# Steps around the output projection of a hybrid attention layer placed anew, and its block sums moved from VectorE to GpSimd

## The chip, the core and the metric

The kernel runs on one core of a Trainium2 chip. The metric is the device time of one execution in microseconds (us). The core has five engines that run their own instruction queues beside one another and wait for each other by semaphores: TensorE (PE, matmuls and transposes; PEld is its weight load), VectorE (DVE), ScalarE (ACT), GpSimd (POOL) and SyncE (SP), which here does nothing but issue DMAs. POOL and ACT issue some DMAs too.

## The reference, cut to what matters

One decoder layer on 2048 tokens of width 1024, all float32. Two kinds of heads share one input projection: gated linear attention (GLA) and dilated sliding-window attention with three branches (window, dilation). Their outputs, side by side, go through the output projection `w_out`, which is where most of the change stands; a normalized MLP of width 4096 follows.

```python
def rmsnorm(x, g):
    return x * rsqrt(mean(x * x, -1) + EPS) * g

nx = rmsnorm(h, attn_norm_g)
gq, gk, gv, gr, glow, dq, dk_, dv_ = split(nx @ w_in)
glog = log_sigmoid(glow @ gla_gate_w2 + gla_gate_b) / 16
o_a = gla_mixer(gq, gk, gv, glog)                  # 4 heads, chunks of 64 tokens
o_a = rmsnorm(o_a, gla_norm_g) * silu(gr)
o_b = dilated_mixer(dq, dk_, dv_, rel_bias)        # 8 heads, (128,1) (512,4) (2048,16)
h = h + concat(o_a, o_b) @ w_out
nm = rmsnorm(h, mlp_norm_g)
h = h + square(relu(nm @ w_ff1)) @ w_ff2
return rmsnorm(h, final_norm_g)
```

## The kernel before, in words

**Arithmetic.** Each float32 operand of a large matmul is split into a high and a low part: ACT rounds the high part (L543), DVE subtracts it to get the low part (L544), and PE runs three matmuls (L140 to L142). A "split" below is this pair of instructions; PE cannot start on an operand before both have run. Many matrix products are done with Strassen-like products of quarter blocks, which need sums of blocks of the operands.

**Stages.** The input projection runs to about 503 us; then attention and GLA, interleaved, to about 849 us; then the output projection to about 1035 us, the first MLP product to about 1645 us and the second to the end.

**Attention and GLA.** The attention is cut into `units`; in each turn of the loop one unit computes scores (L982), DVE adds the bias and takes the row minimum (L992), ACT takes the exponential (L993), PE transposes (L1002), ACT copies (L1009), and PE multiplies with `v` (L1021). The queries of a head and branch are packed by POOL (`pack_q`, L935). `gla_steps` puts a GLA step between units: loads L1148 to L1150, matmuls L1175 and L1199, copies L1201 and L1212 on ACT, transposes L1211. Everything else that shall run meanwhile is listed with `at_unit(n, f, ...)`, which calls `f` at unit `n`.

**Preparation of the output weights.** `sum_wo(c)`, a generator, is called every second unit from unit 8 on, six times for each of four `c`: it loads two rows of blocks of `w_out` into a slot `wtsum` (L1275), has ACT scale one half by `gn`, the GLA norm's weights (L1277), then has POOL make four differences (L1281), and stores them to `wtD`. `mix_wo(c)` loads them again as `wtraw` (L1291) and splits them into four operands `wb`. `load_wo` loads other blocks as they are (`woraw`, L1265) and splits them.

**The output projection.** `mixD` in DRAM holds the attention outputs; `load_mix(p)` brings those of two blocks of 128 rows into `mx` (four DMAs, L1494), written by the last stores of combined attention (`cmb`, L1098 and L1110) and GLA. The first four blocks of 128 rows (`at` = 0 to 3, in the prediction block 0 to block 3, or the first to the fourth plain block) are computed without Strassen products: `plain_rows` splits their part of `mx` into `mT`, PE multiplies, DVE adds the residual `xh` (L1728). From `g` = 14 on, `product0(g)` runs seven products for each pair of blocks, with operands `mcomb` that `prep0` makes three products ahead (sums L1656 and its neighbours on DVE, then a split). `row_done` stores the new rows (L1664) and puts two kinds of entries on a list, `norms`; `next_norm` takes one entry at a time:

- `norm_row`: square-sum of the row by ACT (L1433, which writes its squares into `scr`, half of the one slot `gs`), the root (L174, L175), the scaled row by DVE into `scr` (L1435), eight transposes by PE (L1440), copies by ACT (L1441) into the slot `bb`, and stores to `hTD` (L1428). `scr` is one buffer: the next row's square-sum cannot start before this row's transposes have read it.
- `norm_sums`, after every second row: four differences of the 128x512 pieces in `bb` on DVE (L1448 to L1451), and four stores.

**What sets the order.** The program is traced in the order in which the code is written, and a list scheduler with a timeline of its own then orders each engine's queue; the code pins only a few instructions (`keep_in_program_order`). Buffers come from a pool of 25 rotating slots, so an allocation in another place can move other waits too. An engine runs its queue strictly in order: an instruction that waits holds all that stand behind it, and a DMA that waits on SP's queue holds the DMAs behind it.

## Time and profile before

| | before |
|---|---|
| median of 3 runs | 2224.94 us (2224.32 to 2226.07) |
| the profiled execution | 2224.69 us |
| its span, first to last instruction | 2222.9 us |
| mean granted TensorE clock | 0.994 |
| instructions in the span | 34722 |
| DMA traffic | 499.88 MB, 225 GB/s over the span |

The profile comes from one execution. In its rows, L12 is line 12 of the kernel; `out<-in` names the buffers that an instruction writes and reads; the bracket behind a row of the timeline gives the engine's idle time before it and what ended that. PE, DVE, ACT and POOL are busy time, which leaves out the issuing of DMAs. A granted clock of 1.00 is full speed of TensorE; at 0.50 the same matmul takes twice as long. Small gaps of a busy engine are found in the list of waits and in the windows, not in the shares of busy time: the whole span is 2222.9 us and the waits in question are of 1 to 4 us.

### The profile page before, as it was taken

How to read it: one execution, taken by the hardware profiler on the slowest of the kernel's cores; microseconds unless marked ns; L12 is line 12 of the kernel's file. 1: busy time of each engine (PE TensorE's matmuls, PEld its weight loads, DVE VectorE, ACT ScalarE, POOL GpSimd, SP SyncE). 2: the span in 40 equal slices, each digit the busy share in tenths (PEclk: the TensorE clock that was granted, in tenths of full speed). 3: DMA queues.
4: the chain of work that ended last, by engine and by line, in shares of the span. 5: the costliest groups of instructions: out<-in, count | busy, mean ns of one | idle time of the engine just before them, and what ended most of it. 6: DMA issues, size and time to landing. Idle time of an engine off the chain costs nothing.

```text
span 2222.9 us, 34722 instructions
## 1 busy us (share of the span) xinstructions
PE 2194.7 (99%) x12236; PEld 1905.9 (86%) x12236; DVE 1686.6 (76%) x3134; ACT 1227.1 (55%) x2388; POOL 609.5 (27%) x667
## 2 busy tenths in 40 slices
PE   9999999999999999999999999999999999999998
PEld 8988998899999997788788888888888888888886
DVE  8678766756787888779776778767787697576788
ACT  7365425537888884446555566555555433333446
POOL 1000300125577683000000000000008443042662
PEclk9999999999999999999999999999999999999999
DMA  6676966777967978978654456454489998687775
GB/s 211 178 219 208 249 202 187 250 232 265 305 221 218 282 241 234 281 246 268 192 159 140 146 172 195 151 180 154 134 294 279 306 295 268 217 267 236 268 262 183
DMA packets 341075, 499.88 MB, mean 225 GB/s; under 512 B 37703, under 2 KB 245210, under 8 KB 329636
## 3 DMA queue, kind: packets, MB, share of 16 engines
q1 hardware_dynamic: 300402, 332.88, 47.3%
q0 software_dynamic: 33152, 112.08, 17.9%
q10 hardware_dynamic: 7346, 52.70, 6.3%
q8 instruction: 96, 1.57, 0.3%
q14 instruction: 79, 0.65, 0.1%
HBM read 339.45 MB, written 162.85 MB: 226 GB/s over the span
## 4 chain that ended last, share of the span: by engine, by line
PE 74%; issue 15%; DMA 4%; DVE 4%; ACT 1%; POOL 1%; SPq 1%; POOLq 0%; DVEq 0%; ACTq 0%
PE ps_a L141 7%; PE ps_a L140 7%; PE ps_a L142 7%; PE ps_c L141 6%; PE ps_c L142 6%; PE ps_c L140 6%; PE ps_a L1021 4%; PE ps_d L141 4%; PE ps_d L140 4%; PE ps_d L142 4%; PE ps_o L140 3%; PE ps_o L141 3%; PE ps_o L142 3%; PE ps_d L1002 3%; PE ps_c L984 2%
## 5 line engine op out<-in xcount | busy, mean ns | idle before, releaser
L543 ACT ACTIVATE cb<-bs 128x1024 fp32r<-128x1024 f32 x104 | 110.2, 1060 | 284.5 <-PE ps_o L141 108.7
L544 DVE TENSOR_TENSOR cb<-bs,cb 128x1024 fp32r<-128x1024 f32 x104 | 158.4, 1524 | 123.3 <-ACT cb L543 122.8
L544 DVE TENSOR_TENSOR mcomb<-w1raw,mcomb 128x512 fp32r<-128x512 f32 x224 | 153.6, 686 | 98.4 <-ACT mcomb L543 98.4
L1819 POOL TENSOR_TENSOR bs<-bs,rb 128x1024 f32<-128x1024 f32 x60 | 165.7, 2763 | 200.2 <-DMA bs<-w_ff 195.2
L1535 POOL DMA_DIRECT2D w1raw<-w_ff x64 | 48.1, 752 | 592.5 <-DVE mcomb L544 565.7
L543 ACT ACTIVATE mcomb<-w1raw 128x512 fp32r<-128x512 f32 x224 | 140.2, 627 | 89.0 <-PE ps_c L142 26.5
L1021 PE MATMUL ps_a<-v,pt 128*128 128x65 f32 x1200 | 178.6, 256 | 4.4 <-ACT pt L1009 3.3
L1021 PEld LDWEIGHTS ps_a<-v,pt 128*128 128x128 f32 x1200 | 173.8, 196 | 6.7 <-ACT pt L1009 3.9
L993 ACT ACTIVATE pe<-pe,O 128x256 f32<-128x256 f32 (+1 forms) x384 | 155.4, 454 | 22.4 <-DVE O L992 20.9
L992 DVE CUSTOM_DVE_ANT_0 pe<-ps_c,nb 128x256 f32<-128x256 f32 (+1 forms) x384 | 125.6, 359 | 40.1 <-PE ps_d L1002 18.5
L1002 PE MATMUL ps_d<-ident,pe 128*128 128x128 f32 x600 | 154.9, 280 | 0.2 <-ACT pe L993 0.2
L304 ACT ACTIVATE wcomb<-wraw 128x512 fp32r<-128x512 f32 (+2 forms) x119 | 90.5, 761 | 114.4 <-PE ps_a L141 45.3
L544 DVE TENSOR_TENSOR ca<-ra,ca 128x1024 fp32r<-128x1024 f32 x84 | 134.2, 1598 | 0.1
L140 PE MATMUL ps_c<-hb,mcomb 128*128 128x512 f32 x320 | 124.5, 390 | 1.2 <-DVE acc L1621 1.2
L141 PE MATMUL ps_c<-hb,mcomb 128*128 128x512 f32 x320 | 124.5, 389 | 0.0
L142 PE MATMUL ps_c<-hb,mcomb 128*128 128x512 f32 x320 | 124.2, 389 | 0.0
L140 PE MATMUL ps_c<-cb,ca 128*128 128x512 f32 x312 | 121.4, 389 | 0.0
L141 PE MATMUL ps_c<-cb,ca 128*128 128x512 f32 x312 | 121.4, 389 | 0.0
L142 PE MATMUL ps_c<-cb,ca 128*128 128x512 f32 x312 | 121.4, 389 | 0.0
L306 DVE TENSOR_TENSOR wcomb<-wraw,wcomb 128x512 fp32r<-128x512 f32 (+2 forms) x77 | 72.8, 946 | 48.9 <-ACT wcomb L304 48.7
L1002 PEld LDWEIGHTS ps_d<-ident,pe 128*128 128x128 f32 x600 | 106.6, 184 | 0.7 <-ACT pe L993 0.3
L140 PE MATMUL ps_a<-wcomb,tb 128*128 128x256 f32 (+1 forms) x344 | 98.0, 285 | 0.0
(502 smaller groups left out, 7203.4 us busy)
## 6 DMA issues: line engine op xcount, KB each, us to landing
ra<-actD ACTq DMA_DIRECT2D x50, 1024.0 KB
actD<-ring SPq DMA_DIRECT2D x176, 256.0 KB
rb<-w_ff POOLq DMA_DIRECT2D x84, 512.0 KB, 6.4
bs<-w_ff SPq DMA_DIRECT2D x72, 512.0 KB
w1raw<-w_ff POOLq DMA_DIRECT2D x64, 512.0 KB, 5.1
k<-kD SPq DMA_DIRECT2D x16, 1024.0 KB
rb<-hTD SPq DMA_DIRECT2D x28, 512.0 KB
wraw<-w_in SPq DMA_DIRECT2D x48, 256.0 KB
```

What stands on the lines that cost most here:

```text
L140: T.matmul(out, sh, mh, start=first, stop=False, **kw)
L141: T.matmul(out, sl, mh, start=False, stop=False, **kw)
L142: T.matmul(out, sh, ml, start=False, stop=last, **kw)
L304: A.activation(hi, src, AF.Copy, scale=sc)
L306: V.tensor_tensor(lo, src, hi.bitcast(F32), op=OP.subtract)
L543: A.activation(hi, src, AF.Copy)
L544: V.tensor_tensor(lo, src, hi.bitcast(F32), op=OP.subtract)
L992: V.tensor_tensor_reduce(p, s, bias, scale=1.0, scalar=BIG, op0=OP.add, op1=OP.min, accum_out=nm)
L993: A.activation(p, p, AF.Exp, bias=nm, scale=-1.0)
L1002: T.transpose(pb[:, i * 128:i * 128 + 128], src, ident)
L1021: T.matmul(self.b.opsum[:, n % 4], self.pt[:, i * 128:i * 128 + 128], self.b.v[:, blk, cols], start=first, stop=last)
L1819: (engines or ((G,), (V, V))[len(sums) - 1])[e].tensor_tensor(v, v, r, op=OP.add if op == "+" else OP.subtract)
```

## The change

The numbers of instructions stay, apart from a few waits; 32 subtractions move from DVE to POOL. The parts are:

1. **Last output weights.** The raw blocks of `load_wo(6)` and `load_wo(7)` share one slot.
2. **`sum_wo`** has one more step between its loads and the scaling by ACT. At two units a step, the scaling now comes four units behind the loads instead of two, and the four generators together take 28 steps instead of 24.
3. **Queries.** Those of head 0, branch 1 are packed before the first unit, as those of branch 2 were.
4. **`load_mix(0)`** is called at unit `NU - 9` of the attention instead of behind all units; the functions that it needs are defined further up, unchanged.
5. **`turn_rows`.** The transposes, copies and stores of `norm_row` become a function of their own, called after the next product (or at the next `next_norm`, if that comes first).
6. **`norm_sums`** makes its four differences on POOL (`G`) instead of DVE (`V`).

The core of the diff:

```diff
--- before.py
+++ after.py
+    raws_wo = []
...
     def load_wo(c):
...
-            raw = slot("woraw")[:, :D]
+            if c < 7:
+                raws_wo[:] = [slot("woraw")]
+            raw = raws_wo[0][:, c // 7 * D:c // 7 * D + D]
             SP.dma_start(raw, wo[:, c])
...
     def sum_wo(c):
         raw = slot("wtsum")
         for k in range(2):
             SP.dma_start(raw[:, D * k:D * k + D], wo[:, c + 4 * k])
+        yield
         yield
         A.activation(raw[:, :D], raw[:, :D], AF.Copy, scale=gn[:, c:c + 1])
...
-    for part in range(4):
-        pack_q(0, 2, part)
+    for br in (2, 1):
+        for part in range(4):
+            pack_q(0, br, part)
...
-                for part in range(4) if first else ():
+                for part in range(4) if len(units) > 4 else ():
                     at_unit(first - 4 + part, pack_q, b.h, br, part)
...
     NU = len(units)
-    sums_wo = [x for c in range(4) for x in [sum_wo(c)] * 6]
+    sums_wo = [x for c in range(4) for x in [sum_wo(c)] * 7]
     for n, x in enumerate(sums_wo):
         at_unit(8 + AHEAD + 2 * n, next, x)
     for i in range(8):
         at_unit(NU - 28 + 3 * i + AHEAD, load_wo, (4, (1, 0), (12, 0), 5, (1, 1), (12, 1), 6, 7)[i])
+    at_unit(NU - 9 + AHEAD, load_mix, 0)
...
-    norms = []
+    norms, turning = [], []
...
     def norm_row(h, t):
...
         V.scalar_tensor_tensor(scr, h, r, gM, op0=OP.mult, op1=OP.mult)
-        k = t % HT // 4
-        for q in range(2):
-            pv = view(ps("c"), (4, 128))
-            for c in range(4):
-                T.transpose(pv[:, c], scr[:, (4 * q + c) * 128:(4 * q + c + 1) * 128], ident)
-            A.activation(hb4[2 * k + q], pv, AF.Copy)
-        store_T(t, *(((1, 0), (2, 1)) if k == 0 else ((3, 3),)))
+        turning.append(t)
+
+    def turn_rows():
+        while turning:
+            t = turning.pop(0)
+            k = t % HT // 4
+            for q in range(2):
+                pv = view(ps("c"), (4, 128))
+                for c in range(4):
+                    T.transpose(pv[:, c], scr[:, (4 * q + c) * 128:(4 * q + c + 1) * 128], ident)
+                A.activation(hb4[2 * k + q], pv, AF.Copy)
+            store_T(t, *(((1, 0), (2, 1)) if k == 0 else ((3, 3),)))
...
     def norm_sums(t, x):
         b11, b21, b12, b22 = hb4
         t2, t4, t3 = [view(v, (4, 128)) for v in (x[:, 0, :512], x[:, 0, 512:], x[:, 1, :512])]
-        V.tensor_tensor(b12, b12, b11, op=OP.subtract)
-        V.tensor_tensor(t2, b22, b12, op=OP.subtract)
-        V.tensor_tensor(t4, b21, t2, op=OP.subtract)
-        V.tensor_tensor(t3, t2, b11, op=OP.subtract)
+        G.tensor_tensor(b12, b12, b11, op=OP.subtract)
+        G.tensor_tensor(t2, b22, b12, op=OP.subtract)
+        G.tensor_tensor(t4, b21, t2, op=OP.subtract)
+        G.tensor_tensor(t3, t2, b11, op=OP.subtract)
...
     def next_norm():
+        turn_rows()
         if norms:
...
-    load_mix(0)
     nxt = plain_rows(0, 0)
     for at in range(4):
...
         next_norm()
+        turn_rows()
         row_done(p, e)
...
         product0(g)
+        turn_rows()
         if i in (0, 1, 5):
             next_norm()
...
         product1(at)
+        turn_rows()
         if at in (1, 2, 4):
             next_norm()
```

Three places show how the scheduler's order moves. In these rows the number is the line of the kernel, and xN counts equal rows.

SP's queue at the first loads of `sum_wo`, early in the attention (`nb` is a bias table of a branch, `qs`, `k` and `v` its operands); before:

```order
L913 DMA nb_4799<-rbD_110 128x256
L893 DMA v<-vD 128x16x128
L667 DMA qs<-qD_86 128x2048
L672 DMA k_5060<-kD_90 128x1x2048
L1275 DMA wtsum<-w_out 128x1024 x2
L672 DMA k_5130<-kD_90 128x1x2048
```

and now:

```order
L913 DMA nb_4804<-rbD_110 128x256
L893 DMA v<-vD 128x16x128
L1149 DMA gla<-gqD 128x2x128
L1150 DMA gla<-gkD 128x2x128
L667 DMA qs<-qD_86 128x2048
L913 DMA nb_4804<-rbD_110 128x256
L672 DMA k_5060<-kD_90 128x1x2048
L913 DMA nb_4804<-rbD_110 128x256
L1279 DMA wtsum<-w_out 128x1024
```

Two `gla` loads and two `nb` loads have moved ahead of the `wtsum` loads, which themselves are now parted by an `nb` load.

SP's queue from the last output weights to the second `mx`, at the border of attention and output projection; before:

```order
L1265 DMA woraw<-w_out 128x1024
L1110 DMA mixD_105<-gla 128x4x128
L1265 DMA woraw<-w_out 128x1024
L1494 DMA mx<-mixD_104 32x4x448 x4
L1517 DMA xh<-x 128x1024 x2
L1704 DMA gs<-mlp_norm_g 128x1024
L1494 DMA mx<-mixD_104 32x4x448 x2
L1517 DMA xh<-x 128x1024 x2
L1291 DMA wtraw<-wtD 128x1024 x2
L1110 DMA mixD_105<-gla 128x4x128
```

and now:

```order
L1269 DMA woraw<-w_out 128x1024 x2
L1110 DMA mixD_105<-cmb 2048x1x64
L1392 DMA mx<-mixD_104 32x4x448 x4
L1110 DMA mixD_105<-gla 128x4x128 x2
L1530 DMA xh<-x 128x1024 x2
L1717 DMA gs<-mlp_norm_g 128x1024
L1098 DMA mixD_105<-cmb 2048x1x32
L1392 DMA mx<-mixD_104 32x4x448 x2
L1530 DMA xh<-x 128x1024 x2
L1296 DMA wtraw<-wtD 128x1024 x2
```

The two `woraw` loads follow each other, the first four `mx` loads stand ahead of the GLA stores, and both GLA stores and a store of L1098 now stand ahead of the second `mx` and of the first `wtraw`.

ACT's queue at the third plain block (with buffer numbers: `xh_9778` before and `xh_9777` now hold the rows of the first two blocks, `mT_9869` and `mT_9868` are the third block's operand); before:

```order
L543 ACTIVATE wb5_9804<-wtraw_9801 128x512
L543 ACTIVATE wb6_9807<-wtraw_9801 128x512
L543 ACTIVATE wb4_9810<-wtraw_9801 128x512
L543 ACTIVATE wb7_9813<-wtraw_9801 128x512
L543 ACTIVATE mT_9869<-mx_9793 128x512
L543 ACTIVATE mT_9869<-mx_9793 128x384
L1433 ACTIVATE gs_9762,stats_80<-xh_9778 128x1024
```

and now:

```order
L1468 ACTIVATE gs_9766,stats_80<-xh_9777 128x1024
L174 ACTIVATE stats_80<-stats_80,pair_77 128x1
L175 ACTIVATE stats_80<-stats_80 128x1
L1468 ACTIVATE gs_9766,stats_80<-xh_9777 128x1024
L543 ACTIVATE wb5_9803<-wtraw_9800 128x512
L174 ACTIVATE stats_80<-stats_80,pair_77 128x1
L543 ACTIVATE wb6_9806<-wtraw_9800 128x512
L543 ACTIVATE wb4_9809<-wtraw_9800 128x512
L543 ACTIVATE wb7_9812<-wtraw_9800 128x512
L543 ACTIVATE mT_9868<-mx_9792 128x512
```

The square-sums of both rows of the first pair now stand ahead of the four `wb` splits and of the third block's `mT` split.

More of the change, by code (lines that the diff above doesn't have):

```diff
@@ L1375, in emit, with load_mix, mix_of, by_quarter @@
             was = b
+    tiles = [8 * half + i + 4 * k for half in range(2) for i in range(4) for k in range(2)]
+    mxs, xhs = {}, {}
+    def load_mix(p):
+        if p < 8:
+            u = mxs[p] = view(slot("mx"), (4, 512))
+            half, i = divmod(p, 4)
+            for g in range(4):
+                m = mixD[half][:, 4 * i + g]
+                n = 448 if half == 0 else 512
+                (SP, G)[g % 2 if p else 0].dma_start(u[32 * g:32 * g + 32, :, :n], bass.AP(
+                    tensor=m.tensor, offset=m.offset, ap=[[16 * 512, 32], [32 * 16 * 512, 4], [1, n]]))
+    def mix_of(p, e, q):
+        if q:
+            return mxs[p][:, :, 256:].rearrange("p g (c e t) -> p e c g t", e=2, t=32)[:, e]
+        return mxs[p][:, :, :256].rearrange("p g (e c t) -> p e c g t", e=2, t=32)[:, e]
+    def by_quarter(v):
+        return v.rearrange("p c (g t) -> p c g t", g=4)
+    def kept_on_chip(p):
+        if p < 4:
+            pv = ps("c")
+            for e in range(2):
+                T.transpose(pv[:, 128 * e:128 * e + 128], outs[3, 0][:, tiles[2 * p + e], 1:129], ident)
+            A.activation(mxs[p][:, :, 448:].rearrange("p g (e t) -> p e g t", e=2), view(pv, (2, 4, 32)), AF.Copy)
     NU = len(units)
-    sums_wo = [x for c in range(4) for x in [sum_wo(c)] * 6]
+    sums_wo = [x for c in range(4) for x in [sum_wo(c)] * 7]
     for n, x in enumerate(sums_wo):
@@ L1482, in token_pieces @@
         return step
-    tiles = [8 * half + i + 4 * k for half in range(2) for i in range(4) for k in range(2)]
-    mxs, xhs = {}, {}
-    def load_mix(p):
-        if p < 8:
-            u = mxs[p] = view(slot("mx"), (4, 512))
-            half, i = divmod(p, 4)
-            for g in range(4):
-                m = mixD[half][:, 4 * i + g]
-                n = 448 if half == 0 else 512
-                (SP, G)[g % 2 if p else 0].dma_start(u[32 * g:32 * g + 32, :, :n], bass.AP(
-                    tensor=m.tensor, offset=m.offset, ap=[[16 * 512, 32], [32 * 16 * 512, 4], [1, n]]))
-    def mix_of(p, e, q):
-        if q:
-            return mxs[p][:, :, 256:].rearrange("p g (c e t) -> p e c g t", e=2, t=32)[:, e]
-        return mxs[p][:, :, :256].rearrange("p g (e c t) -> p e c g t", e=2, t=32)[:, e]
-    def by_quarter(v):
-        return v.rearrange("p c (g t) -> p c g t", g=4)
-    def kept_on_chip(p):
-        if p < 4:
-            pv = ps("c")
-            for e in range(2):
-                T.transpose(pv[:, 128 * e:128 * e + 128], outs[3, 0][:, tiles[2 * p + e], 1:129], ident)
-            A.activation(mxs[p][:, :, 448:].rearrange("p g (e t) -> p e g t", e=2), view(pv, (2, 4, 32)), AF.Copy)
     def load_x(p, pin=False):
```

## The prediction

> **What bounds the kernel now.** The page comes first, then the list of what TensorE (PE) waited for, then windows round each of those waits.
>
> ```profile
> PE 2194.7 (99%) x12236; PEld 1905.9 (86%) x12236; DVE 1686.6 (76%) x3134; ACT 1227.1 (55%) x2388; POOL 609.5 (27%) x667
> ```
>
> PE is busy for 2194.7 of 2222.9 us. The change removes no matmul, so it can only win idle time of PE (28 us in all) and time at a lower clock. The wait list says where the idle time sits (total us, times, longest us):
>
> ```profile
> PE ps_a L1021 <- ACT pt L1009: 3.3, 3, 1.3
> PE ps_c L1440 <- DVE gs L1435: 3.2, 1, 3.2
> ...
> PE ps_o L1175 <- ACT gla L1212: 2.1, 1, 2.1
> PE ps_a L140 <- ACT mT L543: 1.6, 1, 1.6
> ...
> PE ps_c L982 <- POOL qp L935: 1.0, 1, 1.0
> PE ps_a L140 <- ACT mcomb L543: 0.7, 1, 0.7
> ```
>
> The windows (start:end, length, busy us of PE, PEld, DVE, ACT and POOL, granted clock, DMA share, GB/s) show what a wait costs beyond itself:
>
> ```profile
> 512.00:524.00 12.00, 12.00 (x114) 11.89 (x114) 9.80 (x42) 6.50 (x16) 4.82 (x8) 1.00 1.05 380
> 524.00:528.00 4.00, 2.72 (x27) 2.52 (x26) 1.63 (x7) 4.00 (x10) 2.86 (x3) 1.00 1.05 368
> 604.00:607.30 3.30, 1.18 (x7) 1.02 (x7) 1.04 (x5) 2.94 (x8) 1.72 (x2) 1.00 1.18 319
> 607.30:614.10 6.80, 6.80 (x32) 6.41 (x31) 3.48 (x10) 5.07 (x16) 5.96 (x9) 0.50 0.95 366
> 842.00:849.75 7.75, 4.03 (x33) 3.47 (x33) 5.12 (x9) 5.33 (x16) 2.43 (x6) 0.99 1.06 282
> 849.75:856.30 6.55, 6.52 (x19) 5.51 (x20) 5.95 (x18) 3.64 (x14) 4.70 (x10) 0.50 1.06 255
> 922.00:924.65 2.65, 0.44 (x2) 0.02 (x1) 2.65 (x5) 2.55 (x6) 0.00 (x0) 1.00 1.04 279
> 924.65:931.50 6.85, 5.86 (x18) 5.00 (x19) 4.71 (x7) 1.96 (x4) 0.00 (x0) 0.50 1.07 341
> ```
>
> After 2.1 us of idle (604), 3.7 us in pieces (842 to 849.75) and 3.2 us (922) the clock stands at 0.50 for some 6.8 us, which costs half of PE's busy time there: 3.4, 3.3 and 2.9 us. The 1.28 us of idle at 524 has no such stretch behind it. So the price of a wait is its length, and about 3.4 us more once it is long.
>
> By the Trainium skill ("TensorE: Matmul & The Clock Gate", Part 1: The HAM clock gate) the clock falls only after an idle window of about 3.4 us. The trace disagrees: 2.1 us was enough at 604. What this rule of the Trainium skill would give is part of the first rival.
>
> **The change part by part.** Times are those of the run before; signs are changes of the span.
>
> *Queries of head 0, branch 1, cast ahead.* At 509.7 PE waited 1.0 us (L982, above) for POOL's casts of these queries. They now run before the input projection ends, where POOL idles. **-1.0.**
>
> *The weight sums (`sum_wo`).* The extra step puts four instead of two units between a load and the ACT split that needs it. What stands behind a late split on ACT's queue is late with it. The first load, in the rows of SP, ACT and PE in the timeline:
>
> ```profile
> 514.04 1.25 SPq L1275 DMA_DIRECT2D wtsum<-w_out  x2
> 523.91 1.15 ACT L1277 ACTIVATE wtsum<-wtsum,stats 128x1024 f32<-128x1024 f32 x1 [3.74 <-DMA wtsum<-w_out]
> 524.97 1.19 ACT L993 ACTIVATE pe<-pe,O 128x256 f32<-128x256 f32 x3
> 526.68 0.44 PE L1021 MATMUL ps_a<-v,pt 128*128 128x65 f32 x2 [1.28 <-ACT pt L1009]
> ```
>
> The split still stands behind the 30th exponential, but two `gla` and two `nb` loads of 128 KB each (512 KB) have moved ahead of the load on SP. DMA is saturated here (380 GB/s, share 1.05, above), so it lands 1.4 us later, at 525.3. Behind the split now stand two exponentials and L1201, on which PE's L1211 waits: 1.06 for the split (524.97 - 523.91), 0.85 for the exponentials, 0.5 for L1201 and 0.1 for the hand-over put that at 527.8. PE reaches its wait at 526.68 - 1.28 = 525.4, less 1.0 for the casts, plus 0.4 (eight 128-column GLA matmuls more ahead of it, four score matmuls fewer): 524.8. Idle 3.0, and 0.4 more at the next L1021, against 1.28: +2.1; with the load no later than now +0.7. At 3 us I take the clock with it, as at 604: +3.4, or 0 if it holds. **+5.5** (0.7 to 5.5).
>
> The fourth load is the one behind the gap at 604 (first the chain of waits, then the timeline; the last two rows are the second load):
>
> ```profile
> 591.51 12.76 DMA wtsum<-w_out
> 604.36 1.15 ACT L1277 ACTIVATE wtsum<-wtsum,stats 128x1024 f32<-128x1024 f32 x1 [3.32 <-DMA wtsum<-w_out]
> 523.95 1.55 SPq L1275 DMA_DIRECT2D wtsum<-w_out  x2
> 531.24 1.15 ACT L1277 ACTIVATE wtsum<-wtsum,stats 128x1024 f32<-128x1024 f32 x1 [1.19 <-DMA wtsum<-w_out]
> ```
>
> It waited behind 2 MB of `qs` and `v` issued within the microsecond before. Now only `gla` loads stand right ahead of it; the `qs`, `v` and `k` are 9 us of matmuls earlier. The load at 523.95 took 7.3 us. ACT reaches the split 44 PE instructions (4.3 us) plus some 1.5 us after the queue moves on, 5.2 us after the issue; 3.4 us of matmuls less 1.6 us of ACT work cover 1.8 us more. So 7.0 us cost nothing and 7.3 cost 0.3 to 0.5. Both the 2.1 and the 3.4 go: **-5.0** (-5.5 to 0).
>
> *Shared slot of the last output weights and the early `load_mix(0)`.* The start of the output projection idles 3.7 us in pieces:
>
> ```profile
> 833.62 3.33 SPq L1265 DMA_DIRECT2D woraw<-w_out  x1
> ...
> 838.86 2.10 SPq L1494 DMA_DIRECT2D mx<-mixD  x4
> 841.16 1.06 ACT L543 ACTIVATE wo<-woraw 128x1024 fp32r<-128x1024 f32 x1 [2.19 <-DMA woraw<-w_out]
> ...
> 849.10 1.04 ACT L543 ACTIVATE mT<-mx 128x512 fp32r<-128x512 f32 x2 [1.29 <-DMA mx<-mixD]
> ```
>
> Before, the first `woraw` held SP for 3.3 us, then came a GLA store, the second `woraw` and `mx`. Now the second follows the first at once and the GLA store comes behind `mx`; I estimate that `mx` goes out 2.8 us earlier, near 836, held by the score matmul that frees its slot. The DMA share is 1.06, with the same bytes queued, so it lands 1.5 to 3 us earlier, at 846 to 847.6. The first `mT` matmul ran 0.7 us behind 849.1; without the 3.7 us of waits PE wants it at 846.0. GLA's L1199 stands behind both `mT` splits on ACT (0.9 us). I count 2.7 us left of 3.7, and the clock still falling: **-1.0** (-6.2 if `mx` lands by 845.5, so that 0.9 is left and the clock holds).
>
> What is late next is the third plain block. In program order on SP, `xh`, the second `mx` and `wtraw` now come behind the last GLA store and the L1098 store. On ACT, the square-sum of the second block (L1433, now L1468) has moved ahead of four `wb` splits and the `mT` split of the third block. It needs the last matmul of block 1 and the eight transposes after it, and PE's next matmul needs that `mT`. Prices:
>
> ```profile
> 869.10 1.06 ACT L1433 ACTIVATE gs<-xh 128x1024 f32<-128x1024 f32 x1 [3.63 <-DVE xh L1728]
> 870.06 0.19 ACT L1433 ACTIVATION_READ_ACCUMULATOR gs<-xh 128x1 f32 x1
> 871.60 1.15 ACT L543 ACTIVATE wb<-wtraw 128x512 fp32r<-128x512 f32 x2 [1.35 <-DMA wtraw<-wtD]
> 872.65 0.28 ACT L174 ACTIVATE stats<-stats,pair 128x1 f32<-128x1 f32 x1
> ```
>
> Start to start: 1.15 + four splits at 0.53 + 0.2 for L174 + 0.55 for `mT`, and 0.2 for two hand-overs: 4.3 us, then 0.1 for DVE's half. PE has nothing else: 4.4 us idle, longer than any gap now, so 3.4 us of clock: **+7.8** (4.4, if the clock holds, to 11, if `wtraw`, late in the same queue, lands 3 us after the square-sum).
>
> *`turn_rows` and the sums on POOL.* At 922 PE waited 3.2 us for the normalized row, since DVE had waited for `mx` and then ran sums and combines first:
>
> ```profile
> 920.02 0.69 DVE L1656 TENSOR_TENSOR mx<-mx 128x512 f32<-128x512 f32 x1 [2.73 <-DMA mx<-mixD]
> 525.14 1.27 POOL L1281 TENSOR_TENSOR wtsum<-wtsum 128x512 f32<-128x512 f32 x1 [8.17 <-ACT wtsum L1277]
> ```
>
> The transposes now stand a product (some 11 us of matmuls) later and 4 x 0.6 us of sums have left DVE: 3.2 + 2.9 go, **-6.1** (0 if another `mx` wait takes its place). The same sums take POOL 4 x 1.27 = 5.1 us a pair of blocks, in some 19 us in which it otherwise only issues DMAs. They have one cost: SP's seventh `wtraw` load now waits, in queue, behind a store of the third sum.
>
> ```profile
> 896.57 1.31 SPq L1291 DMA_DIRECT2D wtraw<-wtD  x2
> 902.55 1.15 ACT L543 ACTIVATE wb<-wtraw 128x512 fp32r<-128x512 f32 x2 [0.79 <-DMA wtraw<-wtD]
> ```
>
> From the end of block 2: transposes, copy and three sums 5.2, two stores 1.1, 5.9 in flight, two `wb` splits 1.1, `mcomb` 0.6: 13.9, and PE wants `mcomb` at 10.9 + 2.0 = 12.9. With DVE's half I take 1.5 us against today's 0.7 (L140 <- `mcomb`): **+0.8** (0 to 5 with the clock).
>
> **Sum:** -1.0 + 5.5 - 5.0 - 1.0 + 7.8 - 6.1 + 0.8 = +1.0. The profiled run took 2224.69 us (span 2222.9), 0.25 under the median of 2224.94; on the median's scale 2225.9. Gains of 13 and losses of 14 cancel: **no change that can be told**, and 0.2% (4.4 us) is about what a measurement of this kernel can tell from none.
>
> **The rivals.** *Faster: the clock holds and `mx` is in time.* The first load's gap stays without its 3.4 us, as the 1.28 at 524 did, and the start closes to 0.9: 2225.9 - 3.4 - 5.2 = 2217.3. For it: `mx` needs to gain only 3.6 us. Against it: 2.1 us was enough at 604. By that rule of the Trainium skill ("TensorE: Matmul & The Clock Gate", Part 1) both gaps, and the one at 604, would be too short; then only the third block (4.4 us) would lose it. Chance 0.30.
>
> *Slower: the fourth load is late again.* If it takes 9.1 us or more from issue to landing, as at 591 it took 12.8, PE idles 2.1 us behind the split and loses the clock as now: 5.0 comes back, 2230.9. It decides at 7.0 us and costs all of it from 9.1. For it: the first load took 9.9 us at 514. Against it: the `k` loads before it have 9 us to drain. Chance 0.23, a late `wtraw` at the third block (+3) included.
>
> *The change does not do what it says* for `load_mix(0)`: its slot is freed by a late score matmul, so it could go out no earlier than now. That is +1.0 on the forecast, 2226.9, and lies within it. Forecast: 0.47 in all.
>
> **How the numbers follow.** Within 0.2%: 0.47; faster: 0.30; slower: 0.23. The range reaches past the faster rival by 2 us and past the slower one by 3: 2215 to 2234. The forecast's own range is 2221.5 to 2229.
>
> **What would show it.** Right: a PE wait of 4 to 5 us on ACT's `mT` split some 22 us after the first `mT` matmul, with the clock at 0.50 behind it; 3 us behind the first `wtsum` split; none behind the fourth; no PE wait on the transposes; POOL near 650 us busy. Wrong: no such wait at the third block (then some 8 us faster), or a wait on the transposes still there.

## The result, and the profile after

The changed kernel took 2251.10 us (median of 6 runs, 2245.85 to 2256.43), the kernel before 2226.82 us (6 runs): ratio 1.011, 95% interval 1.0091 to 1.013. It is slower by some 24 us. The forecast was 2225.9 us, no change that can be told, with a range of 2215 to 2234.

The profiled execution took 2248.78 us, its span 2247.0 us against 2222.9. Its page gives the busy time of each engine:

```profile
PE 2199.3 (98%) x12236; PEld 1907.2 (85%) x12236; DVE 1681.3 (75%) x3102; ACT 1227.2 (55%) x2388; POOL 664.4 (30%) x699
```

PE has as many instructions as before, and 4.6 us more busy time; 2.8 us of that come from longer stretches at a lower clock. The rest of the 24.1 us is idle. PE's list of waits says where (total us, times, longest us):

```profile
PE ps_a L140 <- ACT mT L543: 6.4, 1, 6.4
PE ps_o L1175 <- POOL gla L1165: 5.6, 1, 5.6
PE ps_o L1211 <- ACT gla L1201: 3.9, 1, 3.9
PE ps_a L140 <- ACT mcomb L543: 3.6, 1, 3.6
PE ps_a L140 <- DVE O L1024: 3.3, 1, 3.3
PE ps_a L706 <- DMA acc<-attn_norm_g: 2.3, 1, 2.3
PE ps_c L1481 <- DVE gs L1470: 2.2, 2, 1.8
```

The first five lines were not there before, or not above 1.6 us. Windows round these five (start:end, length, busy us of PE, PEld, DVE, ACT, POOL, granted clock, DMA share, GB/s), the first two gaps, and what follows each of the five:

```profile
510.00:515.80 5.80, 0.17 (x3) 0.01 (x1) 1.11 (x5) 2.33 (x8) 2.77 (x6) 0.71 0.79 232
515.80:522.60 6.80, 6.80 (x45) 6.44 (x46) 3.13 (x12) 2.09 (x5) 2.17 (x4) 0.75 0.98 271
622.90:627.10 4.20, 0.30 (x4) 0.10 (x2) 0.87 (x6) 1.71 (x3) 3.02 (x6) 0.75 0.54 178
627.10:633.50 6.40, 6.40 (x37) 6.29 (x38) 3.20 (x11) 6.37 (x25) 4.89 (x6) 0.63 0.01 2
867.60:871.00 3.40, 3.37 (x8) 2.67 (x9) 3.40 (x8) 0.00 (x0) 0.00 (x0) 0.53 0.53 135
893.30:899.60 6.30, 6.29 (x18) 4.73 (x19) 4.89 (x9) 3.68 (x9) 0.00 (x0) 0.62 1.02 251
923.50:930.00 6.50, 6.50 (x18) 4.99 (x19) 6.34 (x12) 5.10 (x11) 1.09 (x2) 0.59 0.92 244
```

Behind each gap the clock is lower, but the loss there is 1.6 to 2.7 us (busy time times what is missing from 1), not 3.4: the clock already falls inside the longer gaps (0.71 at 510, 0.75 at 622.9), so part of the low stretch is spent idle, and behind the gap that ends at 867 the stretch is short. Narrower windows show a clock of 0.50 from 512.4 to 519.2, 625.0 to 631.9, 867.4 to 870.8, 891.3 to 898.1 and 922.0 to 928.8, and 1.00 on either side: 6.8 us each time and 3.4 once. In the four gaps of 3.6 to 6.4 us it began 1.9 to 4.4 us after PE went idle, so the loss does not follow the length of the gap.

The kernels can be laid beside one another by when PE reaches the same work. The table has, for the kernel before, the time in us at which PE starts the 101st and the 501st value matmul (L1021), the first matmul on `mT` and the first on `mcomb`, and the span; for the others the difference to it. "Border" is the loss between the last two matmuls. Up to 1.6 us of a column already stands at the first score matmul. e6 shows how far a column moves by itself: PE's order there is that of the kernel before, matmul for matmul, and its columns differ by up to 3.4 us.

| profiled execution | 101st value | 501st | first `mT` | first `mcomb` | span | border | ratio of times to before (95%) |
|---|---|---|---|---|---|---|---|
| before | 536.82 | 654.21 | 849.78 | 900.77 | 2222.9 | | |
| changed | +7.8 | +8.5 | +6.0 | +22.7 | +24.1 | +16.7 | 1.011 (1.0091 to 1.013) |
| e1 without early query casts | +1.3 | -2.4 | +9.6 | +18.1 | +20.8 | +8.5 | 1.0108 (1.0093 to 1.0123) |
| e2 without early `mx` | +9.7 | +14.9 | +11.7 | +15.5 | +21.0 | +3.8 | 1.0084 (1.0064 to 1.0103) |
| e3 without `turn_rows` | +8.1 | +8.9 | +5.9 | +22.1 | +24.3 | +16.2 | 1.0119 (1.0098 to 1.0139) |
| e4 sums on DVE | +8.1 | +9.4 | +6.1 | +17.3 | +18.8 | +11.2 | 1.0095 (1.0078 to 1.0112) |
| e5 early casts alone | +6.9 | +10.0 | +11.0 | +12.8 | +12.8 | +1.8 | 1.0091 (1.0068 to 1.0114) |
| e6 casts moved back | +2.5 | -2.2 | -2.6 | -3.4 | -2.7 | -0.8 | 1.0009 (0.9994 to 1.0024) |
| e7 early `mx` alone | +3.7 | +3.3 | +3.9 | +3.6 | +8.2 | -0.4 | 1.0012 (0.9999 to 1.0024) |
| e8 sums on POOL alone | +2.0 | -1.8 | -0.1 | -0.3 | +5.0 | -0.2 | 1.0033 (1.0021 to 1.0045) |
| e9 extra step alone | +1.1 | -2.0 | +7.0 | +5.9 | +9.8 | -1.2 | 1.005 (1.003 to 1.0069) |
| e10 `turn_rows` alone | +2.6 | -0.6 | -0.4 | -1.9 | -3.5 | -1.5 | 1.0007 (0.9995 to 1.0019) |
| e11 extra step, early `mx` | +3.6 | +3.4 | +15.9 | +28.9 | +36.6 | +12.9 | 1.0152 (1.013 to 1.0174) |
| e12 shared slot, early `mx` | 0.0 | -4.6 | -3.1 | -1.9 | +0.5 | +1.1 | 1.0005 (0.9991 to 1.002) |
| e13 changed, GLA stores by ACT | +8.4 | +7.1 | +4.8 | +7.0 | +12.8 | +2.2 | 1.0076 (1.0053 to 1.0099) |
| e14 changed, square-sums behind | +7.8 | +7.0 | +4.8 | +20.2 | +38.1 | +15.5 | 1.02 (1.0182 to 1.0218) |
| e15 without extra step | +9.4 | +17.7 | +20.1 | +27.7 | +33.6 | +7.7 | 1.0129 (1.0109 to 1.015) |
| e16 before, a spare slot | +2.3 | -1.0 | +6.1 | +5.8 | +7.1 | -0.3 | 1.0055 (1.0039 to 1.0072) |

The kernel before took 2220.5 to 2226.8 us in the different comparisons, so ratios are compared, and the columns are used for places, not for sums. Each row is one execution: those of e2, e7, e11 and e15 are the slowest of their runs (e7: 2232.88 us against a median of 2224.17), those of e14 and e16 the fastest. Against the changed kernel the intervals of e1 to e4, e13 and e15 overlap, so what a part costs there is read from its place in the trace, and the ratio is given beside it. The changed kernel has lost 7.8 us at the 101st value matmul (7.5 of them at the first), stays near that until the output projection, loses 16.7 us there before its first product, and little behind it.

### The profile page after: what moved, and what is told of

Same layout as the page of the kernel before. It is cut to its first block, busy times and chain, and to the rows that moved or that the text cites. A ratio compares the mean times of both kernels' runs of the same rounds, so it can differ in the third digit from the quotient of the medians.

```text
span 2247.0 us, 34732 instructions
## 1 busy us (share of the span) xinstructions
PE 2199.3 (98%) x12236; PEld 1907.2 (85%) x12236; DVE 1681.3 (75%) x3102; ACT 1227.2 (55%) x2388; POOL 664.4 (30%) x699
## 3 DMA queue, kind: packets, MB, share of 16 engines
q0 software_dynamic: 33152, 112.08, 17.7%
## 4 chain that ended last, share of the span: by engine, by line
PE 81%; DMA 7%; DVE 5%; ACT 2%; issue 2%; SPq 1%; POOL 1%; DVEq 0%; ACTq 0%; POOLq 0%
PE ps_a L140 8%; PE ps_a L141 8%; PE ps_a L142 8%; PE ps_c L141 7%; PE ps_c L140 7%; PE ps_c L142 7%; PE ps_d L141 4%; PE ps_d L142 4%; PE ps_d L140 4%; PE ps_o L140 4%; PE ps_o L141 4%; PE ps_o L142 4%; PE ps_a L1021 3%; PE ps_d L1002 2%; PE ps_c L984 1%
## 5 line engine op out<-in xcount | busy, mean ns | idle before, releaser
L544 DVE TENSOR_TENSOR mcomb<-w1raw,mcomb 128x512 fp32r<-128x512 f32 x224 | 158.1, 706 | 102.2 <-ACT mcomb L543 102.1
L1021 PE MATMUL ps_a<-v,pt 128*128 128x65 f32 x1200 | 178.2, 255 | 1.5 <-DVE pt L1011 0.9
L1021 PEld LDWEIGHTS ps_a<-v,pt 128*128 128x128 f32 x1200 | 172.8, 195 | 4.3 <-DVE pt L1011 2.6
L544 DVE TENSOR_TENSOR ca<-ra,ca 128x1024 fp32r<-128x1024 f32 x84 | 122.6, 1460 | 0.1
L1619 ACT ACTIVATE acc<-acc 128x512 f32<-128x512 f32 x96 | 60.6, 631 | 68.3 <-DVE acc L1638 27.6
```

Source lines behind the costliest of these rows:

```text
L544: V.tensor_tensor(lo, src, hi.bitcast(F32), op=OP.subtract)
L1021: T.matmul(self.b.opsum[:, n % 4], self.pt[:, i * 128:i * 128 + 128], self.b.v[:, blk, cols], start=first, stop=last)
```

## The experiments

**e1, the change without its third part.** Edit:

```diff
-    for br in (2, 1):
-        for part in range(4):
-            pack_q(0, br, part)
+    for part in range(4):
+        pack_q(0, 2, part)
...
-                for part in range(4) if len(units) > 4 else ():
+                for part in range(4) if first else ():
```

> The change without its third part: the queries of head 0, branch 1 are cast among the units again. Theory A (their early cast takes the slot in which the bias table nb stood, so that nb's first load waits for a matmul 47 instructions later, some 5.6 us, and every load behind it on SP is late): the wait of 5.6 us at 515.8 and its stretch at clock 0.50 go, the first load of nb goes out near 469.6 instead of 475.2; 8 us faster than the changed kernel, 2243. Theory B (the start is late because the extra step of sum_wo has moved GLA loads ahead of wtsum, as the prediction had it): a wait of 3 us behind the first wtsum split is there with or without the early casts; the time stays at 2251 or falls by 1 to 3 us.

In its place theory A held: the loss at the 101st value matmul is 1.3 us, not 7.8, and `nb` goes out at 470.5. But the time did not fall (1.0108): a new wait of 4.7 us stands at 782, where POOL's cast of a later head waits for its slot, which a store of `cmb` still reads. The timeline of POOL:

```profile
781.30 2.01 POOL L935 CAST qp<-qs 128x512 fp32r<-128x512 f32 x2 [6.05 <-DMA mixD<-cmb]
```

**e2, without its fourth part.** Edit: `load_mix(0)` behind the last unit again.

```diff
-    at_unit(NU - 9 + AHEAD, load_mix, 0)
...
+    load_mix(0)
     nxt = plain_rows(0, 0)
```

> The change without its fourth part: load_mix(0) stands behind the last unit again. Theory A (the early mx brings the first block's matmuls ahead of the attention's last GLA steps and combines, SP then holds xh, the second mx and wtraw behind a GLA store that leaves at 871, and PE waits at 867 for a bank of ps_a and at 893 for mT): both waits go (3.3 + 6.4, with 3.3 at a lower clock behind each) and some 3 to 6 us come back at the first mT matmul; 2251 - 16 + 5 = 2240. Theory B (the wait at 893 comes from turn_rows, whose transposes hold the second square-sum ahead of the mT split): the wait of 6 us on mT stays, only the 867 one goes; 2245 to 2248.

The border lost 3.8 us instead of 16.7, with no wait over 1.3 us on `mT`: theory A, in its place. The total fell by less than that (1.0084, an interval that overlaps the changed kernel's), since this kernel is 6 us later at the first `mT` matmul than the changed one; a wait of 5.3 us for L1201 stands in its attention.

**e3 and e4, without the fifth and without the sixth part.** Edits:

```diff
         turning.append(t)
+        turn_rows()
```

```diff
-        G.tensor_tensor(b12, b12, b11, op=OP.subtract)
+        V.tensor_tensor(b12, b12, b11, op=OP.subtract)
...
```

> The change without turn_rows: norm_row makes its transposes at once, as before the change. Theory A (turn_rows takes away the wait of the transposes for the normalized row, 3.2 us and 2.9 at a lower clock, and touches nothing else): that wait is back behind the first products; 2251 + 6 = 2257. Theory B (with the sums on POOL, DVE is early enough for the transposes, and turn_rows gains nothing): no wait on the transposes over 1 us; 2251.

> The change without its sixth part: the four differences of norm_sums on DVE again. Theory A (on POOL they cost 1.3 to 1.7 us each and their third store holds the seventh wtraw load on SP until 915.8, so PE waits 3.6 us for mcomb at 923 and loses 3 us of clock): that load goes out 2 to 3 us earlier, the wait falls to about 1 us or none, 2251 - 6 = 2245, if the transposes don't wait again. Theory B (beside the sums, DVE's own operations take twice as long, 1.36 against 0.68 us for a split, and PE pays for that all through the output projection): the time falls by 10 us or more, to 2241. Theory C (DVE is what the products wait for, and the sums on it bring the wait back): 2251 to 2256.

e3 came out as its theory B in time: `turn_rows` gains nothing here (1.0119 against 1.011); its waits on the transposes are 1.1 us at 946 and 1.8 at 1037, of which the changed kernel has the second too. e4 came out as A at its place: 5.4 us less at the first `mcomb` matmul, and the transposes did not wait again. But another `mcomb` wait of 2.9 us stands at 944, and the ratio of 1.0095 overlaps the changed kernel's.

**e5 and e6, the early casts alone.** Edits to the kernel before: the loop over `br` of the change, and, in e6, the same casts called behind the loop that loads `nb` and `v`.

> The kernel before with the third part of the change alone: the queries of head 0, branch 1 are cast ahead of the units, in the place where the change casts them. Theory A (their slot is the one in which nb stood, nb's first load waits 5.6 us longer): the first load of nb goes out 5 to 6 us later, PE waits some 5 us for L1175 behind POOL's copies of nb and loses 3 us of clock: 7 to 8 us slower than before (ratio 1.0035). Theory B (the start is late only together with the extra step of sum_wo): no such wait, 1 us faster or the same (ratio 0.9995 to 1.0).

> As e5, but the slot of these queries is asked for behind those of the three bias tables and the first v, so that nb keeps its slot; the casts still come ahead of the first unit. Theory A (slot order): nb's first load goes out as before the change, the wait at the start is gone, and so is the 1.0 us for the casts: ratio 0.999 to 1.0. Theory C (it is the eight casts in a row on POOL, 11 us, that delay the copies of nb behind them): the start is late as in e5, ratio 1.0035.

e5: theory A at the start (PE waits 4.7 us for L1175; SP's first `nb` load goes out at 475.2 instead of 469.2), and more than it: 1.0091, with waits of 1.7, 1.9 and 2.4 us later in the attention and 5.5 us for `mcomb`. One part alone makes most of the change's loss. e6 does not test its theories: its casts are late again, PE's order is that of the kernel before, and so is the time (2223.01 us, 1.0009, 0.9994 to 1.0024). It serves as a measure of how far the columns scatter.

**e7 and e8, the early `mx` alone and the sums on POOL alone.**

> The kernel before with the fourth part of the change alone: load_mix(0) at unit NU - 9. Theory A (the early load itself orders ACT and SP anew, so that block 2's mT split and its weights come late): a wait on mT of 4 us or more at the third plain block and 3 us of clock behind it, less the 3 to 6 us that the first mT matmul gains: 2 to 5 us slower than before (ratio 1.001 to 1.002). Theory B (it takes the later attention that the other parts cause to turn the early load into a loss, since there the first block's matmuls run ahead of the last GLA steps): here they don't, the start of the output projection gains 3 to 6 us and nothing is lost behind it: ratio 0.997 to 0.999.

> The kernel before with the sixth part alone: the four differences on POOL. Theory A (the store of the third one holds the seventh wtraw load on SP): PE waits 2.5 to 4 us for mcomb at the first product with the clock behind it, 5 to 7 us, and the transposes' wait of 3.2 us shrinks or stays: 0 to 6 us slower (ratio 1.0 to 1.003). Theory B (DVE beside POOL takes twice its time and PE pays all through the projection): 8 us slower or more (1.0035). Theory C (DVE is relieved of 2.4 us where the normalized row is late, and POOL has time): the transposes' wait goes with its clock, 4 to 6 us faster (0.9975).

e7 loses nothing at the border, but gains nothing either (1.0012, with an interval that includes 1): nearer to theory A's number, with B's picture. e8 is 1.0033: PE waits 2.0 us for `mcomb` instead of 0.7 and 1.6 us for the transposes instead of 3.2, as theory A has it; its span grows behind the first products, by 5 us, as theory B expected of it in kind; PE waits there 1.7 us for a normalized row at 1016, and 0.7 to 1.2 us for `mcomb` at 1044, 1062 and 1096.

**e9 and e10, the extra step alone and `turn_rows` alone.**

> The kernel before with the second part alone: the extra step of sum_wo. Theory A (as the prediction's two terms on sum_wo, with the sizes seen in e1: the fourth wtsum split comes in time and its 2.1 us with the clock go, while the first one costs PE no more than before): 3 to 6 us faster, ratio 0.997 to 0.999. Theory B (the extra step orders POOL's casts of a later head behind a store of cmb, as at 782 in e1, where PE waited 4.7 us and lost 3 us of clock): 8 us come on top: ratio 1.001 to 1.003.

> The kernel before with the fifth part alone: turn_rows. Theory A (the prediction's term: the transposes stand a product later and no longer wait for the normalized row at 922): 3.2 us and 2.9 us of clock go, ratio 0.9973. Theory B (the wait moves: the next square-sum, held by the transposes that now come later, makes the next row late, and a wait on the transposes or on mcomb takes its place): ratio 0.999 to 1.001.

e9: both theories in their places. The gap at 604 is gone (1.3 us late at the 251st value matmul, 1.4 early at the 451st, with a wait of 1.2 us for L1199 between them) and the first split costs 0.7 us instead of 1.3; but at 783 PE waits 5.7 us for a cast behind the store of `cmb`, and loses 9 us with the clock: 1.005. e10 has theory B's number, but not its mechanism: the wait of the transposes is not moved, it is still there. PE's and DVE's rows in e10:

```profile
918.67 0.69 DVE L1662 TENSOR_TENSOR mx<-mx 128x512 f32<-128x512 f32 x1 [2.71 <-DMA mx<-mixD]
924.29 1.03 PE L1474 MATMUL ps_c<-ident,gs 128*128 128x128 f32 x5 [3.38 <-DVE gs L1463]
```

The normalized row is late because DVE waits for `mx`, and the scheduler left the transposes where they were.

**e11 and e12, two parts together.** Edits to the kernel before: parts two and four, parts one and four.

> The kernel before with the second and the fourth part, in which the square-sum of the second plain block stands ahead of the third block's mT split on ACT, as in the changed kernel, while the last matmuls of the attention stay ahead of the output projection's first. Theory A (that square-sum is what holds the third block): PE waits 4 us or more for mT at the third block with 3 us of clock behind it: 7 us over the sum of the two parts alone. Theory B (the wait comes from wtraw and mx, late on SP behind a GLA store, and needs the shared woraw slot): no wait over 2 us there, and the time is that of the two parts alone, ratio 1.0 to 1.002.

> The kernel before with the first and the fourth part, in which the output projection's first matmuls stand ahead of the attention's last ones on PE, as in the changed kernel, while the third block's mT split stays ahead of the second square-sum on ACT. Theory A (in the changed kernel the wait of 3.3 us at 867 comes from the attention's last rows, which DVE copies out of a bank of ps_a only behind a combine): that wait of 2 to 4 us with its 3 us of clock is here, and none over 2 us on mT at the third block: ratio 1.002 to 1.004. Theory B (both waits hang on the early mx as such): 6 us on mT as well: ratio 1.005 or more. Theory C (neither is here): ratio 0.998 to 1.0.

e11 lost 12.9 us at the border (waits of 6.3 us for a combine and 5.8 us for `mT`), 34 us in all: far more than its parts alone. e12 lost 1.1 us and measured 1.0005, nearest to theory C, with 1.6 us of wait for DVE's copy (L1024). So the second square-sum's place, or SP's queue, which differ between the two as well, decides. In e11 the last GLA store leaves SP at 882.4, 16.7 us after the first `mT` matmul; in e12 3.5 us after it. e13 and e14 tell the two apart.

**e13 and e14, the changed kernel with one of the two taken away.** Edits:

```diff
-            SP.dma_start(*x[1])
+            (x[1][2] if len(x[1]) > 2 else SP).dma_start(*x[1][:2])
...
-                        view(flat, (4, 128)))
+                        view(flat, (4, 128)), A if t >= NT - 2 else SP)
```

```diff
-        A.activation(scr, h, AF.Square, accum_out=ss)
+        ins = A.activation(scr, h, AF.Square, accum_out=ss)
+        if t in tiles[:4]:
+            tc.keep_in_program_order(ins)
```

> The changed kernel, with the last two GLA stores issued by ACT instead of SP, so that xh, the second mx and wtraw stand behind no GLA store on SP. Theory A (SP, held by that store until 871, makes the third plain block late): xh goes out before 860, no wait over 2 us for mT at the third block; 6.4 us and 3.3 of clock go: ratio to before 1.0065 instead of 1.011. Theory B (the wait is made on ACT alone, by the square-sum ahead of the splits): here the scheduler has put the square-sum behind the mT split too, so B gives the same for this kernel, and e14 tells the two apart. Theory C (neither: DVE's late combines hold the block): the wait stays at 4 us or more, ratio 1.01.

> The changed kernel, with the square-sums of the first four blocks kept in the order of the code on ACT, so that the second one stands behind the third block's mT split; SP's queue is as in the changed kernel. Theory A (SP): wtraw still lands near 890, PE still waits 3 to 5 us there and loses the clock: 2 us gained at most, ratio 1.010. Theory B (ACT's order, as the prediction had it): the wait falls under 2 us, ratio 1.0065.

e13: the border loses 2.2 us instead of 16.7, the waits of 3.3 and 6.4 us are gone, and only 1.6 us is left on `mT`. In e13 the scheduler also put the second square-sum behind the split, which is why e14 is needed. SP's rows in e13:

```profile
847.99 0.85 SPq L1530 DMA_DIRECT2D xh<-x  x2
...
849.41 1.09 SPq L1392 DMA_DIRECT2D mx<-mixD  x2
...
853.99 3.14 SPq L1296 DMA_DIRECT2D wtraw<-wtD  x2
```

e14: the square-sum stands behind, and PE still waits 6.05 us for `mT`. ACT, with nothing ahead of the split, sat idle for 13 us, since `wtraw` was not there; SP had been held by the GLA store (the first row is ACT's, the others SP's):

```profile
888.35 0.63 ACT L543 ACTIVATE wb<-wtraw 128x512 fp32r<-128x512 f32 x1 [13.21 <-DMA wtraw<-wtD]
855.74 14.85 SPq L1110 DMA_DIRECT2D mixD<-gla  x2
870.68 0.95 SPq L1532 DMA_DIRECT2D xh<-x  x2
```

SP makes the third block late, not ACT's order. That e14 is slower than the changed kernel (1.02) comes behind the first product, where `mcomb` and the normalized rows are late several times (1.5 to 2.9 us).

**e15 and e16.** Edits: `sum_wo` in six steps in the changed kernel; in the kernel before, a slot that is written with one column at the place of the early casts and read at unit 12.

```diff
+    spare = slot("spare")
+    G.tensor_copy(spare[:, :1], pairs[0][0][:, :1].bitcast(F32))
...
+    at_unit(12, lambda: G.tensor_copy(spare[:, 1:2], spare[:, :1]))
```

> The change without its second part: sum_wo in six steps. Theory A (extra step and early mx together make the loss of 17 us between the first mT matmul and the first product, since alone or with the shared slot the early mx costs 3 us at most and e11 lost 23 us over them): that stretch loses 0 to 5 us against before, the start still 8: ratio 1.004 to 1.006. Theory B (the late start and the sums on POOL make the border late by themselves): ratio 1.009 to 1.012.

> The kernel before, with one more slot taken where the early queries of the change take theirs, written with one column and read once; the queries are cast where they were. Theory A (the slot is what makes nb late): nb's first load waits for the same later matmul as in the changed kernel, goes out 5 to 6 us later than before, and PE waits 3 to 6 us in the first 25 us of the attention, with its clock: ratio 1.002 to 1.004. Theory C (the eight casts in a row on POOL make it): no such wait, ratio 1.0 to 1.001. Theory D (late nb costs only because the early casts also bring the first GLA matmuls ahead of the first 20 value matmuls on PE, which they don't here): nb is late, and PE waits less than 2 us more than before; ratio 1.0 to 1.001.

e15: the border lost 7.7 us, not 16.7 and not 0 to 5; the last GLA store there leaves 9.4 us after the first `mT` matmul. The whole was no faster than the changed kernel (1.0129, overlapping intervals), with 20 us lost before the border: theory A failed on the total. e16: one more slot alone puts `nb`'s first load at 475.0, and PE waits for the casts behind the late copies of `nb` (POOL, then PE):

```profile
510.32 0.60 POOL L916 COPY nb<-nb 128x256 f32<-128x256 f32 x1 [10.17 <-DMA nb<-rbD]
512.04 0.33 PE L982 MATMUL ps_c<-k,qp 128*128 128x128 f32 x1 [3.60 <-POOL qp L935]
```

That is 3.6 us against 1.0 before. At the first value matmul e16 is 3.8 us late, the changed kernel 7.5; at the 101st it is 2.3 us late, no more than e6, the changed kernel 7.8. So the slot explains why `nb` is late, but not by itself what the start loses. As in the kernel before, 40 value matmuls stand ahead of the first L1175 on PE in e16; in the changed kernel and in e5 none does. That this order makes the rest, as theory D had it, is argued: no run changes it alone. The ratio of 1.0055, outside D's, is lost later: the trace has 3.5 us of wait for L1201 at 610, and is 6.1 us late at the first `mT` matmul.

**e17 and e18, a version that might beat both.** The kernel before, and e12's kernel, with the last two GLA stores issued by ACT.

> The kernel before, with the last two GLA stores issued by ACT, as in e13. Theory A (SP's queue at the border costs only where a GLA store stands ahead of the loads of the first plain blocks): before the change one GLA store parted the two woraw loads; without it mx goes out 2 to 3 us earlier, and of the 3.7 us of waits and 3.3 of clock at the start of the output projection 2 to 6 us go: ratio 0.997 to 0.999. Theory B (DVE and ACT are what the start waits for): ratio 1.0 to 1.001.

> The kernel before with the first and the fourth part (shared woraw slot, early mx) and the last two GLA stores issued by ACT: the parts of the change that cost nothing where the border is not late, with the queue that e13 points to. Theory A: the first mT matmul comes 3 to 6 us earlier than before and nothing is lost up to the first product: ratio 0.997 to 0.999, faster than both kernels. Theory B (what the border gains, the transposes' wait at the first products takes back): ratio 1.0 to 1.001.

e17 measured 0.9992 (0.9974 to 1.0011): no difference that can be told, and an interval that covers both theories; before the change the loads of the first blocks stood ahead of the second GLA store anyway. e18 measured 1.0047 (1.0028 to 1.0067): slower; PE waits 3.9 us for `mcomb`. No version here measurably beats the kernel before.

## Why the prediction was wrong

It priced the right kinds of loss, and missed two causes: what a new buffer displaces, and what SP's queue holds. By place, forecast and then measured (changed kernel against the one before, to some 3 us, as e6 shows): the start of the attention +4.5 (-1.0 and +5.5) and +7.8; from there to the first `mT` matmul -6.0 (-5.0 and -1.0) and -1.8; from there to the first `mcomb` matmul +8.6 (+7.8 and +0.8) and +16.7; behind it -6.1 and +1.4. Every stretch came out later than forecast.

**The casts (-1.0): the step that failed first.** The step "they now run before the input projection ends, where POOL idles" counted POOL's time alone. The eight casts do run in idle time, but their result takes a slot of the rotating pool, the one that `nb` had. SP's first `nb` load waits for a matmul 47 instructions later. SP before, then SP, POOL and PE after:

```profile
469.21 6.03 SPq L913 DMA_DIRECT2D nb<-rbD  x12
```

```profile
475.23 0.80 SPq L913 DMA_DIRECT2D nb<-rbD  x2
469.50 11.10 POOL L935 CAST qp<-qs 128x512 fp32r<-128x512 f32 x8 [10.55 <-PE ps_a L141]
486.90 0.66 POOL L919 COPY nb<-nb 128x256 f32<-128x256 f32 x1 [4.76 <-PE ps_a L142]
512.88 0.60 POOL L916 COPY nb<-nb 128x256 f32<-128x256 f32 x1 [10.38 <-DMA nb<-rbD]
515.01 0.72 POOL L1165 TENSOR_TENSOR gla<-gla 128x256 f32<-128x256 f32 x1
```

The casts end at 480.6 and POOL idles before it copies `nb`: they do not stand in the way. The loads are 6.0 us late, POOL's copy of the last bias waits for its load, and the GLA operand stands behind it on POOL. On PE, L1175 now comes ahead of the first value matmuls, and waits 5.6 us for it. e1 and e5 show that the casts make this loss, e16 that their slot makes `nb` late; how much of it PE's new order adds stays open.

**The first `wtsum` load (+5.5): wrong.** PE had no wait over 0.6 us behind that split; in e9, without the late start, it waited 0.7 us.

**The fourth load (-5.0): its rival came true in the changed kernel.** The step that failed is the time from issue to landing, taken as 7.3 us. SP, then ACT and PE:

```profile
612.44 3.31 SPq L1279 DMA_DIRECT2D wtsum<-w_out  x2
625.36 1.15 ACT L1282 ACTIVATE wtsum<-wtsum,stats 128x1024 f32<-128x1024 f32 x1 [4.90 <-DMA wtsum<-w_out]
627.05 0.69 PE L1211 MATMUL ps_o<-ident,gla 128*128 128x128 f32 x2 [3.90 <-ACT gla L1201]
```

It took 12.9 us from the issue to the split, beyond the 9.1 us from which that rival cost all of it. Without the early casts (e1, e9) the gap did go.

**The start of the output projection (-1.0): waits right, clock wrong.** PE waited 1.6 and 1.2 us there, 2.8 against the forecast's 2.7, but the clock did not fall:

```profile
849.60:856.40 6.80, 5.14 (x40) 4.71 (x41) 6.72 (x12) 3.80 (x11) 6.54 (x7) 1.00 0.42 83
```

The forecast had left the 3.3 us of clock in. Part of the gain is only moved: 24 small attention and GLA matmuls, 16 more than before, run behind the first `mT` matmul (2.6 us).

**The third plain block (+7.8): place right, cause wrong, and the size near it by luck.** The wait is 6.4 us, and 2.4 are lost at a lower clock. The prediction put it to the square-sum ahead of the `mT` split; e14 moves that away and the wait stays, e13 frees SP and it goes. The rows after, SP, then ACT, then PE:

```profile
856.95 14.85 SPq L1110 DMA_DIRECT2D mixD<-gla  x2
871.89 0.96 SPq L1530 DMA_DIRECT2D xh<-x  x2
...
874.04 6.45 SPq L1392 DMA_DIRECT2D mx<-mixD  x2
...
881.72 0.85 SPq L1296 DMA_DIRECT2D wtraw<-wtD  x2
889.41 0.63 ACT L543 ACTIVATE wb<-wtraw 128x512 fp32r<-128x512 f32 x1 [1.35 <-DMA wtraw<-wtD]
891.07 1.67 ACT L543 ACTIVATE wb<-wtraw 128x512 fp32r<-128x512 f32 x3 [0.84 <-DMA wtraw<-wtD]
893.31 1.22 PE L140 MATMUL ps_a<-wb,mT 128*128 128x512 f32 x2 [6.43 <-ACT mT L543]
```

The first row is two stores, the second of which waited on SP until 871.4 for the last GLA step, and `xh`, the second `mx` and `wtraw` behind it. The second `mx` then took SP 6.4 us more, against 1.1 in e13; what held it is open. The prediction named that order on SP, but kept "late `wtraw`" as an upper bound.

**A wait that was not foreseen** stands in the same place: 3.3 us at 867 and 1.6 of clock. PE needs the bank of `ps_a` that holds the attention's last rows; DVE copies them out (L1024) behind a combine whose small operations ran beside POOL's. DVE's rows, then POOL's:

```profile
861.74 0.90 DVE L1066 TENSOR_TENSOR small<-small 128x8 f32<-128x8 f32 x1
862.68 1.23 DVE L1065 TENSOR_TENSOR small<-small,cmb 128x8 f32<-128x8 f32 x1
863.94 1.19 DVE L1066 TENSOR_TENSOR small<-small 128x8 f32<-128x8 f32 x1
867.16 0.42 DVE L1024 COPY O<-ps_a 128x260 f32<-128x260 f32 x1
862.58 1.29 POOL L1220 TENSOR_TENSOR gla<-gla 128x512 f32<-128x512 f32 x1
863.83 2.63 POOL L1079 TENSOR_TENSOR O<-O,cmb 128x512 f32<-128x512 f32 x2
```

In e13 this wait is gone too. Whether SP's queue or the order that the scheduler then chose took it away was not tried apart.

**`turn_rows` (-6.1): wrong.** e3 and e10 show no gain. The step that failed is that the transposes would stand a product later. On PE the eight that waited at 922 are started 102 matmuls behind the first on `mcomb` in the kernel before and in e10, and 94 behind it in the changed kernel and in e3, with and without `turn_rows`. The wait at 922 is absent in the changed kernel (it has one of 1.8 us at 1038), but e13, in time at the border, has 3.9 us of it again, with `turn_rows` and the sums on POOL. So it was most likely covered by the late start of the products; no run tries that alone.

**The sums on POOL (+0.8): mechanism nearly right, size wrong**; 3.6 us of wait against 0.7, and 2.7 of clock behind it: 5.6, just over its range of 0 to 5. It is not the third sum's store that holds the seventh `wtraw` load but its slot: that store left at 912.97, and the load waits until 915.81 for DVE's splits of an earlier one, of which two took 1.78 us each beside the sums instead of 0.69 (the row of 4.07 us is these two and one of 0.68 behind the sums). DVE, SP and ACT:

```profile
911.71 4.07 DVE L544 TENSOR_TENSOR wb<-wtraw,wb 128x512 fp32r<-128x512 f32 x3
915.81 0.80 SPq L1296 DMA_DIRECT2D wtraw<-wtD  x2
921.74 1.15 ACT L543 ACTIVATE wb<-wtraw 128x512 fp32r<-128x512 f32 x2 [9.00 <-DMA wtraw<-wtD]
```

**What stays open.** Where taking a part out removed its loss, others appeared (e1, e2, e15): the parts do not add up, and no share of the 24 us belongs to one part alone. Alone, the early casts, the extra step and the sums on POOL lost 0.9, 0.5 and 0.3%, together more than the whole change; the shared slot was not run alone. Why e5, with 6.9 us lost at the start, comes to 1.0091 is shown as a list of later waits, not as a cause. The range failed since every term was bounded by itself, at places where the old trace had a wait; none was left for a buffer or a queue that the trace of before never showed as tight.

## What to carry to other kernels

Price a step that is made earlier by three things: its engine's time, the buffer that it takes from a shared pool (who had that one, and when the next comes free), and the place of its DMAs in the issuing queue. A DMA that waits for a late result holds every load behind it on the same engine's queue; give such a store to a queue that has nothing urgent behind it, but check that something gains from it (e13 does, e17 does not). A wait that vanishes may only be covered by a later start: look for it again when the lateness is gone.

## What of the hardware was unexpected

A 128x8 operation on DVE takes 0.16 us, and 0.9 to 1.2 us beside a 128x512 operation of POOL with its 1.1 to 1.3 us, with operands in SBUF; the kernel before has five such too (0.7 to 1.3 us). A 128x512 split went from 0.69 to 1.78 us beside POOL's sums, which themselves took 1.28 to 2.27 instead of 1.27. The Trainium skill ("SBUF — State Buffer", Who interferes with whom) says that a DVE instruction with two SBUF inputs contends with a GpSimd instruction that reads SBUF, because its second input comes through a read interface that both share, and that this contention is an exclusive lock. The trace agrees: the small operations lasted nearly as long as the POOL operation beside them. Work moved from DVE to POOL was not free for DVE: the 32 differences took 21.9 us on DVE and 50.1 on POOL, and DVE's busy time fell by 5.3 us only.

The granted clock fell inside the long gaps of PE, as the windows above show, and all five waits over 3 us of the changed kernel have a lower clock behind them, that of 3.3 us at 867 included (0.53). The price of a gap of 3.6 to 6.4 us here is its length and 1.7 to 2.7 us, not 3.4 more, since the 6.8 us at 0.50 began inside the gap. Gaps of 1.6 and 1.2 us close together (850 and 856) had no low clock behind them.
